# Operand slots at multiples of 128 bytes, the mixing ahead of the second value projection, and varied stationary offsets in four gate pairs

## The chip, the cores and the metric

The kernel runs on one core of a Trainium2 chip, in one launch. The metric is the device time of the launch in microseconds (us), the median of several executions. One further execution was recorded by the hardware profiler, and every row below is from it. TensorE is called PE, VectorE DVE, ScalarE ACT, GpSimd POOL, and SyncE SP; SP issues the DMAs.

## The reference

One layer of a hybrid model on T = 1024 tokens of width 1024, all in float32. `x @ w_in` gives the inputs of three branches: attention over compressed, selected and windowed keys (A), spatial gating (B), and a chunked mLSTM with four heads (C). What is around the change:

```python
def _spatial_gating(u, v, ln_g, ln_b, w_s, b_s):        # branch B
    u = jax.nn.gelu(u)
    v = _layernorm(jax.nn.gelu(v), ln_g, ln_b)
    v = v.reshape(bsz, t_len // CHUNK_B, CHUNK_B, G_B, CH_B)
    w = w_s * jnp.tril(jnp.ones((CHUNK_B, CHUNK_B), w_s.dtype))
    mixed = jnp.einsum('gts,bcsge->bctge', w, v) + b_s.T[:, :, None]
    return u * mixed.reshape(bsz, t_len, D_B)
...
# branch C: q, k through a causal convolution over 4 tokens, gates i and f per token,
# per head 8 chunks of 128 tokens, each with a carried state
...
g = jax.nn.sigmoid(m_g).reshape(bsz, t_len, N_BRANCH, D_MODEL)
merged = g[:, :, 0] * (y_a @ w_br_a[i]) + g[:, :, 1] * (y_b @ w_br_b[i]) + g[:, :, 2] * (y_c @ w_br_c[i])
r = ALPHA * x + merged @ w_out[i]
r = r + jax.nn.sigmoid(r @ ple_gate[i]) * (p[i] @ ple_w[i])
x = _layernorm(r, ln_g[i], ln_b[i])
```

## The kernel before

**Products.** Each float32 operand is split into a high part in a rounded matmul format (fp32r) and the remainder as a low part in the same format. A product of two operands is three matmuls: high by high, low by high, high by low. Each matmul has its own weight load, which runs beside the matmul ahead of it. The kernel has 7135 matmuls, most of them with a moving operand of 512 columns; the program names them by the line that issues them: L130 (projections, the products of the branches, and the output product), L139 (values and gates of the attention, 288 columns), L151 (projections in token order, 256 columns), L786 (Strassen products), L1050 and L1090 (last gate).

**Stages in order of time.** The attention with the projections woven into it takes the time to about 491 us. From there the values of branch B and branch C are projected by `proj_tok256` (L151): the first value projection (weights `wtm[0]`, `wtm[1]`, 384 matmuls) goes through a gelu into `vb`, the second (`wtm[2]`, `wtm[3]`, 384 matmuls) is copied to `vs` and stored to the DRAM scratch `v1scr` (L714, L716). In the same stretch the sums of x that Strassen's method needs (`xraw`, L652 to L658, with their split `split_op`, L643) and the gate recurrences of branch C are computed: `gi`, `gf`, `bc` (L670 to L677), a round trip through DRAM to lay out each chunk's last values (`lastv` to `lscr` to `lrow`, then the scan `mrow`, L689), another for `mp`, and three transposes of them on PE (L706). Then comes the mixing of branch B: L722 is a matmul for its bias, and eight chunks follow, each one with four matmuls (L741, two passes each in the records), four scaled additions on DVE from PSUM (L744) and four products with the gate in `yb` (L747). `yb` is stored to `ysc[1]`. Then 20 Strassen products follow from about 601 to 1040 us. Each is 7 products of 12 matmuls at L786, 84 in all, 1680 for the 20. The stationary operand of each is one slot of `sh` (high, L772, ACT) and `sl` (low, L773, DVE), the moving operand is a part of `xhs`/`xls` or of a sum. Of the 20, 12 are gate pairs (`mg_pair`), the last four of which (q = 8 to 11) come after the heads. The chunk recurrences of each head (L920 to L970) are woven into the others. The branch products, the output product, and the last gate end the kernel.

**Order.** The framework's scheduler takes instructions in the order in which the program was written as their priority, and each engine then runs its own list strictly in order, with semaphores between engines.

**Slots.** On-chip buffers are laid out one after another in the order in which pools are opened, each at a multiple of 32 bytes. `ident` takes 512 bytes of a partition, and `vec`, 53 columns of 4 bytes, takes 224 in its slot; so all later slots start 96 bytes past a multiple of 128. The `y` slots hold 1032 columns (`YW`, for the four columns of padding of the convolution), 4128 bytes, so each starts 32 bytes further in its line of 128 than the one ahead of it. Worked out from these sizes, the start within 128 bytes of the operands (moving, stationary) is:

| line | matmuls | moving | stationary |
|---|---|---|---|
| L130 | 1824 | 96 | 96 |
| L139 | 192 | 0 | 96 |
| L151 | 768 | 96 | 96 |
| L514, L515 (scores of the attention) | | 0 | 0 |
| L786 | 1680 | 96 | 0 |
| L1050 | 432 | 96 | 96 (342), 0 (72), 64 (18) |
| L1090 | | 32 or 64 or 96 | 96 or 32 |

Of the kernel before, what the change touches and what calls it, by code (L numbers as in the profile page):

```python
# [46 lines left out]
def hybrid_kernel(ctx, tc, xm, pT, wfm, wvg, wtm, cmpw1, cmpw2, cpos, vecs, sgwT, sgb,  # L47
# [579 lines left out]
    nc.gpsimd.affine_select(out=wT, in_=wT, pattern=[[0, 4], [1, P]], compare_op=OP.is_ge,
                            fill=0.0, base=0, channel_multiplier=-1)
    ones = pq.tile([P, P], F32, name="ones")
    vv.memset(ones, 1.0)  # L630
    bsb = pq.tile([P, 512], F32, tag="mt", bufs=1, name="bsb")
    nc.sync.dma_start(bsb, sgb.to_broadcast([P, 512]))
# [29 lines left out]


# [46 lines left out]
    v1scr = dr.tile([NH_C, P, NT, P], F32, name="v1scr")  # L710
    for wi in range(2):
        for i, po in enumerate(proj_tok256(wtm[2 + wi], xh, xl)):
            vs = pq.tile([P, 2, 2, P], F32, tag="vs", bufs=2, name="vs")
            nc.any.tensor_copy(out=vs.rearrange("p j a d -> p (j a d)"), in_=po)  # L714
            for a in range(2):
                nc.sync.dma_start(v1scr[2 * wi + a, :, 2 * i:2 * i + 2, :], vs[:, :, a, :])  # L716
    for m in range(2):
        right["T4"][m] = split_op(t4[m], xp, "x", 16)


# [514 lines left out]
```

## Time and profile before

| | |
|---|---|
| median of 3 executions | 1395.22 us (1393.98 to 1396.69) |
| profiled execution | 1394.37 us, its span 1392.6 us |
| PE busy | 1355.7 us, 97% of the span |
| DVE, ACT, POOL busy | 61%, 37%, 11% |
| chain that ended last | PE 85%, DVE 6%, DMA 3%, ACT 3%, issue 2% |

The span is that of the program in the trace; some 1.8 us of the execution's time lie around it. A busy PE counts a matmul from its start to its modelled end, and matmuls overlap, so the pace is read from one start to the next. The chain is followed back from the last instruction, from each to what released it; its shares say which engine the end waited for.

### The profile page before, as it was taken

The numbers are of one execution on the slowest core, as the hardware profiler recorded it, in microseconds if no ns is written. First come the engines' busy times: TensorE is split into PE (matmuls) and PEld (weight loads), VectorE is DVE, ScalarE is ACT, GpSimd is POOL, SyncE is SP. The second block draws the span as 40 slices with busy tenths as digits, with TensorE's granted clock in tenths as the row PEclk, the third lists the DMA queues.
The fourth block names the chain that finished last, engine by engine and source line by source line (L and its number), as shares of the span: only waits on it lengthen the run. The fifth ranks groups of instructions, "written<-read, shape, count | busy, mean of one in ns | idle before, by whom it ended". The sixth has DMA issues, their size and how long they took to land.

```text
span 1392.6 us, 18947 instructions
## 1 busy us (share of the span) xinstructions
PE 1355.7 (97%) x7135; PEld 1134.0 (81%) x7135; DVE 849.4 (61%) x1974; ACT 521.9 (37%) x1040; POOL 158.0 (11%) x181
## 2 busy tenths in 40 slices
PE   9999999999999998889999999999999999999997
PEld 7977888887888998868788787887878887888786
DVE  6236686436777557377776677766454546334755
ACT  6353434243342343135445355454452212223211
POOL 0011211101211100001001000010000344000312
PEclk9999999999999999999999999999999999999999
DMA  8131101111110042333222332235346543113211
GB/s 311 31 84 32 31 24 42 39 46 54 43 64 5 16 153 77 92 106 122 91 61 95 117 108 75 76 121 197 121 141 217 181 157 121 46 61 126 94 38 46
DMA packets 47931, 127.46 MB, mean 92 GB/s; under 512 B 5080, under 2 KB 16216, under 8 KB 47840
## 3 DMA queue, kind: packets, MB, share of 16 engines
q1 hardware_dynamic: 46880, 123.11, 26.8%
q0 software_dynamic: 960, 3.15, 1.0%
q8 instruction: 56, 0.92, 0.3%
q14 instruction: 35, 0.29, 0.1%
HBM read 101.00 MB, written 25.23 MB: 91 GB/s over the span
## 4 chain that ended last, share of the span: by engine, by line
PE 85%; DVE 6%; DMA 3%; ACT 3%; issue 2%; POOL 0%; SPq 0%; DVEq 0%; ACTq 0%; POOLq 0%
PE ps_pj L130 18%; PE ps_a L786 15%; PE ps_b L130 9%; PE ps_b L786 8%; PE ps_o L537 7%; PE ps_g L1050 5%; PE ps_c L786 4%; PE ps_st L514 2%; PE ps_pj L151 2%; PE ps_v L139 2%; PE ps_st L515 2%; PE ps_e L1090 2%; PE ps_st L151 1%; PE ps_s L493 1%; DMA xraw<-in_xm_dram 1%
## 5 line engine op out<-in xcount | busy, mean ns | idle before, releaser
L537 PEld LDWEIGHTS ps_o<-V,pt 128*128 128x128 f32 x912 | 117.6, 191 | 12.1 <-ACT pt L517 3.3
L130 PE MATMUL ps_pj<-xh,whi 128*128 128x512 f32 x288 | 115.5, 401 | 2.3 <-DVE QA L403 2.3
L537 PE MATMUL ps_o<-V,pt 128*128 128x65 f32 x912 | 116.6, 269 | 0.5 <-POOL pt L519 0.3
L130 PE MATMUL ps_pj<-xh,wlo 128*128 128x512 f32 x288 | 114.8, 398 | 0.0
L130 PE MATMUL ps_pj<-xl,whi 128*128 128x512 f32 x288 | 114.5, 398 | 0.0
L517 ACT ACTIVATE pt<-ps_st 128x512 f32<-128x512 f32 x114 | 65.4, 594 | 103.9 <-PE ps_st L515 96.7
L786 PE MATMUL ps_a<-op_hi,sl 128*128 128x512 f32 x240 | 95.2, 397 | 0.0
L786 PE MATMUL ps_a<-op_lo,sh 128*128 128x512 f32 x240 | 95.2, 396 | 0.0
L786 PE MATMUL ps_a<-op_hi,sh 128*128 128x512 f32 x240 | 94.7, 395 | 0.0
L773 DVE TENSOR_TENSOR sl<-ss,sh 128x512 fp32r<-128x512 f32 x80 | 54.8, 689 | 61.8 <-ACT sh L772 58.6
L93 ACT CAST whi<-wraw 128x1024 fp32r<-128x1024 f32 x46 | 48.2, 1048 | 82.7 <-PE ps_b L130 46.9
L130 PE MATMUL ps_b<-sp_hi,wlo 128*128 128x512 f32 x192 | 74.8, 390 | 1.3 <-DVE wlo L94 1.3
L94 DVE TENSOR_TENSOR wlo<-wraw,whi 128x1024 fp32r<-128x1024 f32 x46 | 61.7, 1342 | 22.6 <-ACT whi L93 18.4
L130 PE MATMUL ps_b<-sp_lo,whi 128*128 128x512 f32 x192 | 74.7, 389 | 0.0
L130 PE MATMUL ps_b<-sp_hi,whi 128*128 128x512 f32 x192 | 74.0, 390 | 0.0
L772 ACT CAST sh<-mraw 128x512 fp32r<-128x512 f32 x60 | 37.3, 622 | 82.6 <-PE ps_c L786 33.6
L1005 POOL TENSOR_TENSOR M<-M,gt 128x512 f32<-128x512 f32 x32 | 42.9, 1349 | 203.8 <-issue 174.3
L130 PEld LDWEIGHTS ps_pj<-xh,whi 128*128 128x128 f32 x288 | 54.2, 188 | 13.6 <-PE ps_pj L130 3.9
L130 PEld LDWEIGHTS ps_pj<-xl,whi 128*128 128x128 f32 x288 | 54.2, 188 | 9.8
L130 PEld LDWEIGHTS ps_pj<-xh,wlo 128*128 128x128 f32 x288 | 54.3, 189 | 9.0
L772 ACT CAST sh<-ss 128x512 fp32r<-128x512 f32 x80 | 49.6, 620 | 26.0 <-PE ps_b L786 25.3
L786 PEld LDWEIGHTS ps_a<-op_hi,sl 128*128 128x128 f32 x240 | 45.2, 188 | 11.0
(370 smaller groups left out, 3549.6 us busy)
## 6 DMA issues: line engine op xcount, KB each, us to landing
mraw<-in_wfm_dram SPq DMA_DIRECT2D x40, 512.0 KB, 3.6
gsc<-gt SPq DMA_DIRECT2D x24, 512.0 KB, 2.6
gt<-gsc SPq DMA_DIRECT2D x24, 512.0 KB, 4.1
wraw<-in_wfm_dram SPq DMA_DIRECT2D x18, 512.0 KB, 3.6
xraw<-in_xm_dram SPq DMA_DIRECT2D x14, 512.0 KB, 6.0
yraw<-ysc SPq DMA_DIRECT2D x12, 512.0 KB, 4.4
wraw<-in_wbr_dram SPq DMA_DIRECT2D x12, 512.0 KB, 4.4
wraw<-in_wtm_dram SPq DMA_DIRECT2D x8, 512.0 KB, 3.8
```

The source lines that it names most:

```text
L93: nc.scalar.copy(hi[:, c], raw[:, c])
L94: vv.tensor_sub(lo[:, c], raw[:, c], hi[:, c])
L130: mm(po[:M, :], lhsT=a[:, k, :], rhs=b(k, half), start=(i == 0), stop=(i == n - 1))
L139: mm(po[:, :n], lhsT=tok(a, k, tt), rhs=b[:, k % 4, :], start=(i == 0), stop=(i == tot - 1))
L151: mm(po, lhsT=tok(a, 4 * i + k, tt), rhs=b[:, k, :], start=(i == 0 and tt % 2 == 0 and k == 0 and j == 0), stop=(i == 1 and k == 3 and j = ...
L517: act(pt.rearrange("p h q -> p (h q)"), sp, AF.Exp)
L537: mm(po[:, h * 65:h * 65 + 65], lhsT=pt[:, h, :], rhs=V[:, j, vi, :], start=(first and h == 0), stop=last, skip_group_check=True)
L772: nc.scalar.copy(hi, src)
L773: vv.tensor_sub(lo, src, hi)
L786: mm(bank, lhsT=l[a][:, k, :], rhs=r[b], start=first and k == 0 and i == 0, stop=k == K - 1 and i == 2, skip_group_check=True)
L1005: nc.gpsimd.tensor_add(M[n][:, s], M[n][:, s], t[:, s])
L1050: mm(po[:, 0:n], lhsT=a[k][:, ts_], rhs=b[k][:, s], start=(k == 0 and i == 0), stop=(k == KT - 1 and i == 2))
```

## The change

The change has four parts. First, slots: `vec` is 64 columns wide, the convolution's buffers and `nb` fill whole slots of 4096 bytes, `sh` and `sl` have 544 columns and `ng4` 32. Worked out as above, every moving operand of L130, L151, L786 (L787 after it), L1050 and L1090 and every stationary one starts at 0 within 128 bytes, but for the part that follows; the scores of the attention start at 32 and 32, and L139 at 32 and 0. Second, offsets: in the four last gate pairs the stationary operand starts at 4, 8, 16, 32, 48, 64 or 96 bytes, by the product (`STARTS`, in elements of 4 bytes). Third, the convolution adds shifted slices (1021 to 1023 columns) in place of a padded buffer, and the denominators of the chunks go into a small buffer `dn` by a copy of one column on DVE, 32 of them in all. Fourth, the order of the text: the sums of x (`split_op` and what follows it) stand ahead of the first value projection, and the mixing stands ahead of the second.

```diff
-YW = 1032
+STARTS = dict(B11=4, T1=2, T2=8, B21=16, T3=24, B22=1, T4=12)
...
-    vec = cst.tile([P, 53], F32, name="vec")
+    vec = cst.tile([P, 64], F32, name="vec")
...
-    wT = pq.tile([P, 4, P], F32, name="wT")
-    nc.sync.dma_start(wT, sgwT)
...
-    vb = [pq.tile([P, 2, 512], F32, tag="yc", bufs=4, name="vb") for _ in range(4)]
-    for wi in range(2):
-        for i, po in enumerate(proj_tok256(wtm[wi], xh, xl)):
-            gelu2(vb[i][:, :, wi * 256:wi * 256 + 256], po.rearrange("p (t n) -> p t n", t=2), 512)
...
         right[n] = [(xhs[m + r][j], xls[m + r][j]) for r in range(2)]
 
+    wT = pq.tile([P, 4, P], F32, name="wT")
+    nc.sync.dma_start(wT, sgwT)
...
+    vb = [pq.tile([P, 2, 512], F32, tag="yc", bufs=4, name="vb") for _ in range(4)]
+    for wi in range(2):
+        for i, po in enumerate(proj_tok256(wtm[wi], xh, xl)):
+            gelu2(vb[i][:, :, wi * 256:wi * 256 + 256], po.rearrange("p (t n) -> p t n", t=2), 512)
...
-    v1scr = dr.tile([NH_C, P, NT, P], F32, name="v1scr")
-    for wi in range(2):
-        for i, po in enumerate(proj_tok256(wtm[2 + wi], xh, xl)):
...
     prs = pst("m", 2)
     mm(prs, lhsT=ones, rhs=wT.rearrange("p g t -> p (g t)"), start=True, stop=True)
...
     for i in range(4):
         nc.sync.dma_start(ysc[1][i], yb[i])
 
+
+    v1scr = dr.tile([NH_C, P, NT, P], F32, name="v1scr")
+    for wi in range(2):
+        for i, po in enumerate(proj_tok256(wtm[2 + wi], xh, xl)):
+            vs = pq.tile([P, 2, 2, P], F32, tag="vs", bufs=2, name="vs")
+            nc.any.tensor_copy(out=vs.rearrange("p j a d -> p (j a d)"), in_=po)
+            for a in range(2):
+                nc.sync.dma_start(v1scr[2 * wi + a, :, 2 * i:2 * i + 2, :], vs[:, :, a, :])
+    for m in range(2):
+        right["T4"][m] = split_op(t4[m], xp, "x", 16)
...
-        def left(src):
-            hi = pg_.tile([P, 512], F32R, tag="sh", bufs=3, name="sh")[:, 0:w]
-            lo = pg_.tile([P, 512], F32R, tag="sl", bufs=3, name="sl")[:, 0:w]
+        def left(src, at):
+            hi = pg_.tile([P, 544], F32R, tag="sh", bufs=3, name="sh")[:, at:at + w]
+            lo = pg_.tile([P, 544], F32R, tag="sl", bufs=3, name="sl")[:, at:at + w]
...
-            l = left(src)
+            l = left(src, starts.get(name, 0))
...
-        xq = [yp.tile([P, YW], F32, tag="y", bufs=YB, name="xpad") for _ in range(2)]
-        for t in xq:
-            nc.gpsimd.memset(t[:, 0:4], 0.0)
+        xq = [yp.tile([P, T], F32, tag="y", bufs=YB, name="xq") for _ in range(2)]
...
-        nb = yp.tile([P, NT, 129], F32, tag="y", bufs=YB, name="nb")
+        nb = yp.tile([P, NT, P], F32, tag="y", bufs=YB, name="nb")
+        dn = pq.tile([P, NT], F32, tag="dn", bufs=1, name="dn")
...
-            nc.scalar.copy(nb[:, c, :], pn[:, 0:129])
+            nc.scalar.copy(nb[:, c, :], pn[:, 0:P])
+            vv.tensor_copy(dn[:, c:c + 1], pn[:, P:P + 1])
...
     for q in range(8, 12):
-        mg_pair(q)
+        mg_pair(q, STARTS)
```

What it moves on the engines is seen at three places. The first is PE's list from the transposes of the recurrences to the first Strassen product; before, the second projection runs up to L722 and all of the mixing follows it:

```order
L706 MATMUL ps_m<-ident,gi 128x32
L151 MATMUL ps_pj<-whi,xh 128x256
...
L706 MATMUL ps_m<-ident,bc 128x32
L151 MATMUL ps_pj<-wlo,xh 128x256
L151 MATMUL ps_pj<-whi,xl 128x256
L706 MATMUL ps_m<-ident,gf 128x32
...
L151 MATMUL ps_st<-whi,xl 128x256
L722 MATMUL ps_m<-wT,ones 128x512
L741 MATMUL ps_m<-wT,vb 128x128 x32
L786 MATMUL ps_a<-xh,sh 128x512
```

In the same stretch of the list after the change, L711, L730 and L787 are what L722, L741 and L786 were:

```order
L706 MATMUL ps_m<-ident,gi 128x32
L711 MATMUL ps_m<-wT,ones 128x512
L151 MATMUL ps_pj<-whi,xh 128x256
...
L730 MATMUL ps_m<-wT,vb 128x128 x4
L151 MATMUL ps_st<-wlo,xh 128x256
...
L706 MATMUL ps_m<-ident,bc 128x32
...
L730 MATMUL ps_m<-wT,vb 128x128 x8
L151 MATMUL ps_pj<-wlo,xh 128x256
...
L151 MATMUL ps_st<-whi,xl 128x256
L787 MATMUL ps_a<-xh,sh 128x512
```

The eight chunks of the mixing now stand inside the second projection: 94 matmuls of L151 after L711 comes the first chunk, between chunks stand 6 to 18 more (two chunks stand together), and after the eighth come 210, the last 192 of which are the projection's second half of weights.

The second place is DVE's list ahead of `gi`, which the first transpose on PE reads. Before:

```order
L652 TENSOR_TENSOR xraw<-xraw 128x1024
L673 SCALAR_TENSOR_TENSOR gf<-gf,rt 32x128
L675 MEMSET rt 32x128
L654 TENSOR_TENSOR xraw<-xraw 128x1024
L643 TENSOR_TENSOR op_lo<-xraw,op_hi 128x1024
L655 TENSOR_TENSOR xraw<-xraw 128x1024
L676 SCALAR_TENSOR_TENSOR bc<-gf,rt 32x128
L174 SCALAR_TENSOR_TENSOR ge_a<-ge_a,ps_pj 128x512
L677 TENSOR_TENSOR gi<-gi,bc 32x128
```

After (L640 and L642 are what L652 and L654 were, L631 is L643; the two of x's sums ahead of these rows are left out):

```order
L631 TENSOR_TENSOR op_lo<-xraw,op_hi 128x1024
L643 TENSOR_TENSOR xraw<-xraw 128x1024
...
L94 TENSOR_TENSOR wlo<-wraw,whi 128x1024
L631 TENSOR_TENSOR op_lo<-xraw,op_hi 128x1024
...
L646 TENSOR_TENSOR xraw<-xraw 128x1024
L176 SCALAR_TENSOR_TENSOR vb<-ge_a,ps_pj 128x2x256
L174 SCALAR_TENSOR_TENSOR ge_a<-ge_a,ps_pj 128x512
L676 SCALAR_TENSOR_TENSOR bc<-gf,rt 32x128
L719 BN_STATS s_5335<-vb 128x6
...
L677 TENSOR_TENSOR gi<-gi,bc 32x128
```

From the first of x's sums (L652, L640) to `gi`, before has four passes over 1024 columns, one of 512 and three small ones; after has eight over 1024 (L640, L642, L643, L646, L94 and three of L631), five over 512 (L174, L176), one L719 and three small ones.

The third place is SP's list of DMAs at the end of the second projection. Before:

```order
L822 DMA mraw<-in_wfm_dram 128x1024
L716 DMA v1scr<-vs 128x2x128 x2
L756 DMA ysc_81<-yb 128x1024
```

After:

```order
L745 DMA ysc_84<-yb 128x1024
L823 DMA mraw<-in_wfm_dram 128x1024 x2
L754 DMA v1scr<-vs 128x2x128 x6
L823 DMA mraw<-in_wfm_dram 128x1024
L754 DMA v1scr<-vs 128x2x128 x2
L899 DMA V_6417<-v1scr 128x8x128
```

The last stores of `v1scr` now stand behind those of `yb`. The pool with `wT`, `vb` and `vs` (`pq`) closes behind them, and `sh`, `sl`, `ng4` and `V1` lie in the space that it frees; so the first `sh` waits for the last store out of `vs`, where it waited for the last use of the mixing's buffers.

## Rows read from the trace of the kernel before

**Rows 1.** The page, busy time, share of the span and instructions of each engine.
```profile
PE 1355.7 (97%) x7135; PEld 1134.0 (81%) x7135; DVE 849.4 (61%) x1974; ACT 521.9 (37%) x1040; POOL 158.0 (11%) x181
```

**Rows 2.** Timeline of PE, L130: start, duration (us), line, operation, tiles, shape.
```profile
1099.67 0.39 PE L130 MATMUL ps_b<-sp_lo,whi 128*128 128x512 f32 x1
...
1102.84 0.39 PE L130 MATMUL ps_b<-sp_hi,wlo 128*128 128x512 f32 x1
```

**Rows 3.** Timeline of PE, L786.
```profile
706.42 0.40 PE L786 MATMUL ps_b<-xh,sh 128*128 128x512 f32 x1
...
708.99 0.40 PE L786 MATMUL ps_b<-xl,sh 128*128 128x512 f32 x1
```

**Rows 4.** Timeline of PE, L1050.
```profile
1285.73 0.39 PE L1050 MATMUL ps_g<-gh,sp_hi 128*128 128x512 f32 x1
...
1290.82 0.40 PE L1050 MATMUL ps_g<-gl,sp_hi 128*128 128x512 f32 x1
```

**Rows 5.** Timeline of PE, L151 (256 columns).
```profile
500.08 0.28 PE L151 MATMUL ps_st<-whi,xl 128*128 128x256 f32 x1
...
503.20 0.28 PE L151 MATMUL ps_st<-wlo,xh 128*128 128x256 f32 x1
```

**Rows 6.** Timeline of PE, L139 (288 columns).
```profile
39.71 0.30 PE L139 MATMUL ps_v<-wh,xh 128*128 128x288 f32 x1
...
41.98 0.29 PE L139 MATMUL ps_v<-wh,xl 128*128 128x288 f32 x1
```

**Rows 7.** Timeline of PE, the attention's L514 and L515.
```profile
480.69 0.39 PE L515 MATMUL ps_st<-QB,KBs 128*128 128x512 f32 x1
...
481.15 0.40 PE L515 MATMUL ps_st<-QB,KBs 128*128 128x512 f32 x1
```

**Rows 8.** Timeline of DVE, 517 to 545 us; in brackets the idle time and releaser.
```profile
517.33 1.22 DVE L652 TENSOR_TENSOR xraw<-xraw 128x1024 f32<-128x1024 f32 x1 [3.10 <-DMA xraw<-in_xm_dram]
...
520.00 1.20 DVE L643 TENSOR_TENSOR op_lo<-xraw,op_hi 128x1024 fp32r<-128x1024 f32 x1
...
521.13 1.21 DVE L655 TENSOR_TENSOR xraw<-xraw 128x1024 f32<-128x1024 f32 x1
...
522.60 0.65 DVE L174 SCALAR_TENSOR_TENSOR ge_a<-ge_a,ps_pj 128x512 f32<-128x512 f32 x1
...
523.18 0.27 DVE L677 TENSOR_TENSOR gi<-gi,bc 32x128 f32<-32x128 f32 x1
...
533.61 0.13 DVE L681 COPY lastv<-cm 32x1 f32<-32x1 f32 x1
...
541.19 0.17 DVE L689 TENSOR_TENSOR_SCAN mrow<-lrow 4x8 f32<-4x8 f32 x1 [1.82 <-DMA lrow<-lscr]
...
544.31 1.00 DVE L737 TENSOR_SCALAR vb<-vb,mv,rs_y 128x512 f32<-128x512 f32 x2
```

**Rows 9.** Window: us, PE busy (x), granted clock, DMA share, GB/s.
```profile
546.50:553.30 6.80, 5.05 (x22) 0.50 0.41 121
```

**Rows 10.** Timeline of PE, 527 to 601 us.
```profile
527.65 0.24 PE L706 MATMUL ps_m<-ident,gi 32*128 32x32 f32 x1
...
548.25 0.31 PE L706 MATMUL ps_m<-ident,bc 32*128 32x32 f32 x1 [4.58 <-ACT bc L701]
...
585.34 1.16 PE L741 MATMUL ps_m<-wT,vb 128*128 128x128 f32 x8 [0.41 <-DVE mt L744]
...
593.53 1.16 PE L741 MATMUL ps_m<-wT,vb 128*128 128x128 f32 x8 [0.89 <-DVE mt L744]
...
600.92 0.80 PE L786 MATMUL ps_a<-xh,sh 128*128 128x512 f32 x1 [4.18 <-ACT sh L772]
```

**Rows 11.** Timeline of ACT at 581 and 600 us.
```profile
581.71 0.58 ACT L714 COPY vs<-ps_st 128x512 f32<-128x512 f32 x1 [2.29 <-PE ps_st L151]
...
600.25 0.62 ACT L772 CAST sh<-mraw 128x512 fp32r<-128x512 f32 x1 [17.95 <-DVE yb L747]
```

**Rows 12.** DMA issues, 582.3 to 583.3 us: count, KB each, us to landing.
```profile
v1scr<-vs SPq DMA_DIRECT2D x2, 128.0 KB, 3.8
```

More of the change, by code (lines that the diff above doesn't have):

```diff
@@ L233, in hybrid_kernel @@
     nc.sync.dma_start(ident, identc)
-    nc.sync.dma_start(vec, vecs)
+    nc.sync.dma_start(vec[:, 0:53], vecs)
     pa_ctx = ExitStack()
@@ L624, in hybrid_kernel @@
     pq = pq_ctx.enter_context(tc.tile_pool(name="pq", bufs=1))
-    wT = pq.tile([P, 4, P], F32, name="wT")
-    nc.sync.dma_start(wT, sgwT)
[L627 to L632, printed above, removed]
-    vb = [pq.tile([P, 2, 512], F32, tag="yc", bufs=4, name="vb") for _ in range(4)]
-    for wi in range(2):
-        for i, po in enumerate(proj_tok256(wtm[wi], xh, xl)):
-            gelu2(vb[i][:, :, wi * 256:wi * 256 + 256], po.rearrange("p (t n) -> p t n", t=2), 512)
     def split_op(src, pl_, tg, bf):
@@ L661, in hybrid_kernel @@
         right[n] = [(xhs[m + r][j], xls[m + r][j]) for r in range(2)]
+    wT = pq.tile([P, 4, P], F32, name="wT")
+    nc.sync.dma_start(wT, sgwT)
+    nc.gpsimd.affine_select(out=wT, in_=wT, pattern=[[0, 4], [1, P]], compare_op=OP.is_ge,
+                            fill=0.0, base=0, channel_multiplier=-1)
+    ones = pq.tile([P, P], F32, name="ones")
+    vv.memset(ones, 1.0)
+    bsb = pq.tile([P, 512], F32, tag="mt", bufs=1, name="bsb")
+    nc.sync.dma_start(bsb, sgb.to_broadcast([P, 512]))
+    vb = [pq.tile([P, 2, 512], F32, tag="yc", bufs=4, name="vb") for _ in range(4)]
+    for wi in range(2):
+        for i, po in enumerate(proj_tok256(wtm[wi], xh, xl)):
+            gelu2(vb[i][:, :, wi * 256:wi * 256 + 256], po.rearrange("p (t n) -> p t n", t=2), 512)
     gi = pq.tile([32, P], F32, name="gi")
@@ L708, in hybrid_kernel @@
     vv.tensor_scalar_mul(cols[:, 2, :], pc_[:, 64:96], CS)
-    v1scr = dr.tile([NH_C, P, NT, P], F32, name="v1scr")
-    for wi in range(2):
-        for i, po in enumerate(proj_tok256(wtm[2 + wi], xh, xl)):
[L713 to L718, printed above, removed]
     prs = pst("m", 2)
@@ L761, in hybrid_kernel, with strassen @@
     pq = pg_
-    ng4 = pg_.tile([P, 4], F32, name="ng4")
-    vv.tensor_scalar_mul(ng4, vec[:, C_NG:C_NG + 4], 0.25)
-    def strassen(raw0, raw1, K, right, done):
+    ng4 = pg_.tile([P, 32], F32, name="ng4")
+    vv.tensor_scalar_mul(ng4[:, 0:4], vec[:, C_NG:C_NG + 4], 0.25)
+    def strassen(raw0, raw1, K, right, done, starts={}):
         w = K * P
         a11, a12, a21, a22 = raw0[:, 0:w], raw0[:, w:2 * w], raw1[:, 0:w], raw1[:, w:2 * w]
-        def left(src):
-            hi = pg_.tile([P, 512], F32R, tag="sh", bufs=3, name="sh")[:, 0:w]
-            lo = pg_.tile([P, 512], F32R, tag="sl", bufs=3, name="sl")[:, 0:w]
+        def left(src, at):
+            hi = pg_.tile([P, 544], F32R, tag="sh", bufs=3, name="sh")[:, at:at + w]
+            lo = pg_.tile([P, 544], F32R, tag="sl", bufs=3, name="sl")[:, at:at + w]
             nc.scalar.copy(hi, src)
@@ L814, in hybrid_kernel, with strassen_fm @@
     rawn = [0]
-    def strassen_fm(f0, f1, done):
+    def strassen_fm(f0, f1, done, starts={}):
         tg = ("wraw", "whi")[rawn[0] % 2]
@@ L822, in strassen_fm, with mg_pair @@
             nc.sync.dma_start(t, wfm[f])
-        strassen(raw[0], raw[1], 4, right, done)
-    def mg_pair(q):
+        strassen(raw[0], raw[1], 4, right, done, starts)
+    def mg_pair(q, starts={}):
         gt = [wp.tile([P, T], F32, tag="wlo", bufs=WB, name="gt") for _ in range(2)]
@@ L832, in done @@
             act(gt[i][:, j * 512:j * 512 + 512], bank, AF.Tanh, scale=0.5)
-        strassen_fm(FM["mg"] + 2 * q, FM["mg"] + 2 * q + 1, done)
+        strassen_fm(FM["mg"] + 2 * q, FM["mg"] + 2 * q + 1, done, starts)
         for i in range(2):
@@ L857, in tap @@
                 return vec[:, C_CW + 4 * i + j:C_CW + 4 * i + j + 1]
-            act(r, x[:, 4:4 + T], AF.Identity, scale=tap(3), bias=vec[:, C_CB + i:C_CB + i + 1])
-            for j in range(3):
-                stt(out=r, in0=x[:, 1 + j:1 + j + T], scalar=tap(j), in1=r, op0=OP.mult, op1=OP.add)
+            act(r, x, AF.Identity, scale=tap(3), bias=vec[:, C_CB + i:C_CB + i + 1])
+            for d in (3, 2, 1):
+                stt(out=r[:, d:T], in0=x[:, 0:T - d], scalar=tap(3 - d), in1=r[:, d:T], op0=OP.mult, op1=OP.add)
             for half in range(2):
@@ L953, in hybrid_kernel @@
                 C1 = Cn
-        dn = pq.tile([P, NT], F32, tag="dn", bufs=1, name="dn")
-        stt(out=dn.unsqueeze(2), in0=nb[:, :, P:P + 1], scalar=-1.0, in1=nb[:, :, P:P + 1], op0=OP.mult, op1=OP.max)
+        stt(out=dn, in0=dn, scalar=-1.0, in1=dn, op0=OP.mult, op1=OP.max)
         vv.tensor_max(dn, dn, cols[:, 1, 8 * h:8 * h + 8])
```

2 lines of the change are left out of this document (1 added, 1 removed).

## The prediction

> **What bounds the kernel now.** The page comes first: PE is busy for 97% of the span [rows 1], and the chain that ended last is mostly PE. So two things count: the pace of a matmul behind the one ahead of it, and the few places where PE waits. The pace is read from the timelines, as starts of matmuls far from any interruption, because durations overlap. At L130, with both operands 96 bytes past a multiple of 128, 14 steps take 3.17 us, 226.4 ns each [rows 2]. At L786, same shape, moving operand at 96 and stationary at 0, 11 steps take 2.57 us, 233.6 ns [rows 3]. L1050 in its part with unequal starts takes 5.09 us for 22, 231.4 ns [rows 4]. L151, 256 columns and both at 96, takes 3.12 us for 26, 120.0 ns [rows 5]. From L130 and L151 one column costs (226.4 - 120.0) / 256 = 0.416 ns, and some 13 ns are fixed; the fixed part at L786 is 20. The reader is to see that the two commonest kinds of matmul differ by 7 ns with nothing but their addresses (and the program around them) apart.
>
> The waits come next, in the timeline from 527 to 601 us. PE stands for 4.58 us before a transpose of `bc` [rows 10], and behind it a window of 6.8 us has a granted clock of 0.50 with 5.05 us of PE work in it [rows 9], so the low clock costs 5.05 / 2 = 2.5 us. The mixing goes from chunk to chunk in steps of (593.53 - 585.34) / 4 = 2.05 us, each begun by a wait for DVE's additions, and the first Strassen matmul waits 4.18 us for its `sh`, to start at 600.92 [rows 10].
>
> **Slots.** 1680 matmuls at L786 now read both operands from 0. Of these, 336 are in the four varied pairs. Of the other 1344, about 1150 stand in long runs; there I take the full step from L786 to L130, 233.6 - 226.4 = 7.2, taken as 6.8 because the last digit of the rows (10 ns over 11 and 14 steps) leaves it open by about 1: 7.8 us. The some 196 in between the chunk recurrences are interrupted every few matmuls; for them I take a third, 2.5 ns each, 0.5 us. L1050 and L1090 have about 170 with unequal starts, at 231.4 - 226.4 = 5.0 ns (5.5 with the slower ones at L1090): 0.9 us. L130 and L151 were equal and stay equal: nothing, which holds if equality and not the value 96 is what counts. The attention's operands go from 0 and 0 to 32 and 32, equal as before: nothing. L139 has its operands 96 apart before, in the other direction, and its 17 steps take 2.27 us [rows 6], 133.5 ns; less 288 columns at 0.416 this is 13.7 fixed. So a moving operand at 0 with a stationary one at 96 costs what equal starts cost: the slow case is a moving operand at 96 with a stationary one at 0, or it needs more columns. In either reading 0 with 0 should be fast, but no long run here shows it: the attention's three at 0 and 0 are 0.46 us apart over two steps [rows 7], 230 ns, behind other shapes and not settled. This is the step with the least support. Its bounds are 0 (the pace is the same) and the same 7.2 ns on all 1680, 12.1 us.
>
> **Varied offsets.** 336 matmuls with stationary starts from 4 to 96 bytes, moving at 0. Bounds per matmul: 6.8 ns saved (as L130), or 3.5 lost (half the step again, on top of L786's own); so 2.3 saved to 1.2 lost. By L139's row the 96 should be fast; I take 0.9 saved.
>
> **The Trainium skill's rule here.** Rows 2 and 3 show 226.4 and 233.6 ns for one shape. The Trainium skill says in "TensorE: Matmul & The Clock Gate", section "Step-by-step: what each phase is for", that PE has two independent read ports, one for the moving operand and one for weight loads, so that loading the next weights doesn't take bandwidth from the running matmul; and "SBUF — State Buffer", section "Specifications (TRN2)", gives cachelines of 16 bytes, for which 0, 32 and 96 are alike. By both the starts shouldn't matter, and the time would be 1392.8. The trace disagrees as far as the two rows go, but it can't say that the addresses are the reason.
>
> **The order.** I follow it engine by engine.
> - *gi.* Before, from the landing of the last `xraw` at 517.33 to `gi` at 523.18, DVE does four passes over 1024 columns, 1.13 us from start to start (520.00 to 521.13), a half pass of 0.58 (522.60 to 523.18), and small ones [rows 8]. After, the order has eight full passes, five half ones, one L719 (priced as a half) and the small ones (5.85 - 4 x 1.13 - 0.58 = 0.75): 9.0 + 3.5 + 0.75 = 13.3 us, so `gi` begins at about 530.6 and ends at 530.9. PE comes to its transpose at 527.65 [rows 10] and waits about 3.2 us. Queued behind it are L711 and the second projection.
> - *First chunk.* From there L711 (0.9) and 94 of L151 at 0.12 bring PE to the first L730 at about 543.2. Its `vb` needs the statistics of all chunks and the square root. On DVE these stand partly behind `mrow`, which waits for a round trip through DRAM: `lastv` 533.61, `mrow` 541.19 [rows 8], 7.6 us. With `lastv` at about 533.3 `mrow` comes at 540.8; the statistics left over (2.3, four half passes), the root (3.1, from 541.19 to 544.31) and one normalization (0.5) give 546.8. PE waits 3.6 us. Since this wait ends at 546.8 whatever the one for `gi` does, the first is absorbed in it.
> - *To the end of the projection.* From the first L730 PE has eight chunks of 1.16 [rows 10] and a change of form each (1.2), 290 matmuls at 0.12, and two transposes: about 44.8 us, so it ends at 591.6. DVE needs 2.05 a chunk and 0.54 for the next normalization, 2.6 in all, beside 2.6 to 2.9 on PE, so it hides, just; if it didn't, each chunk would cost PE some tenths, up to 2 us. The 4.58 us wait for `bc` and the mixing's waits for DVE are what goes.
> - *First Strassen product.* What is late next is the last `vs`. Its copy takes 0.58 [rows 11], its store lands 3.8 us after issue [rows 12] (SP's load of `mraw` ahead of it is issued by then), and `sh` takes 0.62 [rows 11]; with the steps between, 5.6 us. L787 begins at about 597.3 instead of 600.92: 3.6 us gained. `ng4` and `V1` wait for the same store, but nothing on PE asks for them for many us.
>
> Bounds: without the wait at the first chunk 3.6 more, 7.2 gained; with the clock falling behind both waits as it did before, twice 2.5, 1.4 lost. The waits are shorter than the 4.58 us that went ahead of the low clock. I take half of one fall, 1.2: **2.4 us gained**.
>
> **Small edits.** The 32 copies of one column on DVE (0.13 us by the `lastv` row [rows 8], 4 us in all) lie beside the Strassen matmuls; DVE is 61% busy. If that cover were gone, the chunk's wait would grow by 0.13, 4 us in all; I take 0.1 lost. The convolution without padding saves two POOL fills per head that PE doesn't wait for: nothing.
>
> **Sum.** 7.8 + 0.5 + 0.9 + 0.9 + 2.4 - 0.1 = 12.4 us. Against the profiled execution (1394.37, span 1392.6 and 1.8 around it) this is 1382.0; the median of three is 0.85 above the profiled one, and against it I say **1382.5**, its own range 1376 to 1388.
>
> **Rivals.** About 0.2%, 2.8 us, is what a measurement of this kernel can tell from no change; so faster is below 1392.4 and slower above 1398.0.
> - *The starts don't matter* (0.13). L786 differs from L130 by its surroundings (ACT writing `sh` and DVE `sl` beside it, other banks), and only the order's 2.4 and the odd 0.1 remain: 1395.2 - 2.4 = 1392.8. For it: L139, unequal and not slow. Against it: L1050, far from the Strassen products, is slow too where its starts are unequal. The two rules of the Trainium skill would make this one.
> - *0 with 0 is a slow pair* (0.11). The attention's 230 ns would be its pace, or up to 231. Then L130 loses 1824 x 4.6 = 8.4 us, L151 768 x 4.6 = 3.5, L1050 and L1090 360 x 4.6 = 1.7; L786 gains 1680 x 2.6 = 4.4, the order 2.4: 6.8 us lost, about **1402**. It decides where the pace p of 0 with 0 passes 229.6 ns: 2952 (p - 226.4) = 1680 (233.6 - p) + 2400. For it: those are the only rows with 0 and 0. Against it: three matmuls behind another shape are no settled run.
> - *Aligned starts take away part of the fixed 13 ns as well* (0.07). If 5 of it went on all 3600 and more in long runs, 18 us more, some 1364. For it: nothing but that the fixed part has to come from somewhere; L139 with its moving operand at 0 has it in full, which is against it.
> - *A new wait eats the gain* (0.07): the mixing's DVE work turns into PE's pace, or the clock falls more often in the woven stretch: 1388 to 1398.
>
> **How the numbers follow.** The forecast has 0.62. The range leaves out the pair of far cases, 0.18: from 1374 (the forecast with all bounds good: 3.6 for the missing wait, 1.4 for the offsets, 1.2 for the clock, 2 for 7.2 ns everywhere) to 1396. Faster: 0.62, half of the first rival, 0.07, and part of the last: 0.77. Slower: the second rival and little else, 0.11. Same: 0.12.
>
> **What would show it.** Right: steps of 227 ns at L787 in the 16 plain products, against 231 to 237 in the four varied pairs, by product; L1050 at 227 throughout; L130 still 226 to 227. PE waiting about 3 us at `gi` and 3 to 4 at the first L730 (at 547), none at `bc`, no DVE waits in the mixing above some tenths, L787 first at 597. Wrong: L787 still at 233, which is the first rival; L130 at 230, the second; L151 below 115, the third; a clock of 0.50 in more than one window between 530 and 600, or chunks over 3.5 us apart, the last.

## The result, and the profile after

The changed kernel takes 1380.99 us (median of 4, 1379.31 to 1382.15), the kernel before 1394.99 on the same chip: a ratio of 0.9897 [0.988, 0.9915], 14.0 us faster. The prediction was 1382.5. The time came out, but not from where the prediction had it.

The page after (span; PE busy; chain by engine), beside [rows 1]:

```profile
span 1379.7 us, 18957 instructions
...
PE 1348.5 (98%) x7135; PEld 1133.2 (82%) x7135; DVE 848.6 (62%) x2006; ACT 521.9 (38%) x1040; POOL 157.9 (11%) x173
...
PE 86%; DVE 6%; DMA 3%; ACT 2%; issue 1%; POOL 0%; SPq 0%; DVEq 0%; ACTq 0%; POOLq 0%
```

The span is 12.9 us shorter with the same instructions on PE. Where they went is read from three starts: the first Strassen product, its end, and the end of the last gate. Before, the first product starts at 600.92 [rows 10] and the branch products behind the last one at 1039.79; after, at 593.30 and 1026.09. So 7.6 us are won ahead of the Strassen products, 438.9 - 432.8 = 6.1 in them; behind them 0.9 are lost.

**Ahead of them.** The timeline of PE after, with the idle time and its releaser in brackets, answers [rows 10]:

```profile
530.07 0.24 PE L706 MATMUL ps_m<-ident,gi 32*128 32x32 f32 x1 [1.82 <-DVE lastv L682]
...
544.75 0.46 PE L730 MATMUL ps_m<-wT,vb 128*128 128x128 f32 x2 [0.61 <-DVE vb L726]
...
587.33 0.28 PE L151 MATMUL ps_st<-whi,xl 128*128 128x256 f32 x1
...
593.30 0.80 PE L787 MATMUL ps_a<-xh,sh 128*128 128x512 f32 x1 [5.69 <-ACT sh L773]
```

The transpose of `gi` waits 1.8 us, the first chunk of the mixing (L730) 0.6, and nothing waits at `bc`. The projection's last matmul starts at 587.33, and the first Strassen matmul stands 5.69 us for its `sh`. The chain behind this on DVE, answering [rows 8]:

```profile
529.74 0.27 DVE L677 TENSOR_TENSOR gi<-gi,bc 32x128 f32<-32x128 f32 x1
...
532.17 0.13 DVE L681 COPY lastv<-cm 32x1 f32<-32x1 f32 x1
...
538.60 0.16 DVE L689 TENSOR_TENSOR_SCAN mrow<-lrow 4x8 f32<-4x8 f32 x1 [1.54 <-DMA lrow<-lscr]
...
544.06 1.00 DVE L726 TENSOR_SCALAR vb<-vb,mv,rs_y 128x512 f32<-128x512 f32 x2
```

`gi` starts at 529.74 where 530.6 was predicted, `mrow` at 538.60 (540.8), the first `vb` at 544.06. The windows (us, PE busy, granted clock, DMA share, GB/s) show what followed each of three waits:

```profile
530.80:533.90 3.10, 3.10 (x15) 0.57 0.01 0
593.30:599.20 5.90, 5.62 (x12) 0.50 0.30 89
1281.00:1286.00 5.00, 5.00 (x15) 0.66 0.30 120
```

The low clock behind `gi`'s wait made PE late, and this lateness took the place of the wait for `vb`, which is why that is only 0.6 us. Behind the 5.69 us wait nothing covers the low clock: it costs 5.62 / 2 = 2.8 us. That isn't all new. The kernel before has a low clock there too, besides the one of [rows 9]:

```profile
597.70:604.50 6.80, 3.58 (x8) 0.50 0.72 277
```

There it costs 3.58 / 2 = 1.8 us. So the first Strassen product takes 22.73 us after and 21.50 before, and 19.44 where the clock doesn't fall (e11, below). The third fall, behind a wait of 2.1 us in the last gate, wasn't there before.

**In them.** The long runs of L787, answering [rows 3], first and last of 12:

```profile
641.10 0.40 PE L787 MATMUL ps_a<-op_hi,sh 128*128 128x512 f32 x1
...
643.67 0.39 PE L787 MATMUL ps_a<-op_lo,sh 128*128 128x512 f32 x1
```

11 steps in 2.57 us: 233.6 ns, as before. Over the 11 steps inside a product the undisturbed ones without varied offsets have 230.6 to 234.5, where before they had 232.5 to 234.3. The step to 226.4 ns on which most of the predicted gain rested is not there, although every operand now starts at a multiple of 128. L1050, in the part of [rows 4], did go to 226 to 227 (2.26 us for 10 steps):

```profile
1275.08 0.39 PE L1050 MATMUL ps_g<-gl,sp_hi 128*128 128x512 f32 x1
...
1277.34 0.39 PE L1050 MATMUL ps_g<-gh,sp_lo 128*128 128x512 f32 x1
```

The gain inside the Strassen products is mostly elsewhere: in the four of them that share PE with a head's chunk recurrences. Before, the first of these takes from 661.88 to 692.42 (below), 30.54 us; after 655.31 to 684.57, 29.26. All four: 122.2 before, 116.8 after. The other 15 gain 1.9 us together, and the first one loses 1.2.

### The profile page after: what moved, and what is told of

Read it like the earlier page. It is cut to its first block, busy times and chain, and to the rows that moved or that the text cites. A ratio compares the mean times of both kernels' runs of the same rounds, so it can differ in the third digit from the quotient of the medians.

```text
span 1379.7 us, 18957 instructions
## 1 busy us (share of the span) xinstructions
PE 1348.5 (98%) x7135; PEld 1133.2 (82%) x7135; DVE 848.6 (62%) x2006; ACT 521.9 (38%) x1040; POOL 157.9 (11%) x173
## 4 chain that ended last, share of the span: by engine, by line
PE 86%; DVE 6%; DMA 3%; ACT 2%; issue 1%; POOL 0%; SPq 0%; DVEq 0%; ACTq 0%; POOLq 0%
PE ps_pj L130 18%; PE ps_a L787 15%; PE ps_b L130 9%; PE ps_b L787 8%; PE ps_o L537 7%; PE ps_g L1050 5%; PE ps_c L787 3%; PE ps_st L514 2%; PE ps_pj L151 2%; PE ps_v L139 2%; PE ps_st L515 2%; PE ps_e L1090 2%; PE ps_st L151 1%; PE ps_s L493 1%; DMA xraw<-in_xm_dram 1%
## 5 line engine op out<-in xcount | busy, mean ns | idle before, releaser
L130 PE MATMUL ps_pj<-xh,whi 128*128 128x512 f32 x288 | 115.6, 401 | 2.3 <-DVE QA L403 2.3
L537 PE MATMUL ps_o<-V,pt 128*128 128x65 f32 x912 | 116.6, 269 | 0.5 <-POOL pt L519 0.3
L130 PE MATMUL ps_pj<-xh,wlo 128*128 128x512 f32 x288 | 114.7, 398 | 0.0
L130 PE MATMUL ps_pj<-xl,whi 128*128 128x512 f32 x288 | 114.5, 398 | 0.0
L787 PE MATMUL ps_a<-op_hi,sl 128*128 128x512 f32 x240 | 95.2, 397 | 0.0
L787 PE MATMUL ps_a<-op_hi,sh 128*128 128x512 f32 x240 | 95.1, 396 | 0.0
L787 PE MATMUL ps_a<-op_lo,sh 128*128 128x512 f32 x240 | 95.1, 396 | 0.0
L130 PE MATMUL ps_b<-sp_hi,wlo 128*128 128x512 f32 x192 | 74.8, 390 | 1.3 <-DVE wlo L94 1.3
L130 PE MATMUL ps_b<-sp_lo,whi 128*128 128x512 f32 x192 | 74.7, 389 | 0.0
L130 PE MATMUL ps_b<-sp_hi,whi 128*128 128x512 f32 x192 | 74.0, 389 | 0.0
L94 DVE TENSOR_TENSOR wlo<-wraw,whi 128x1024 fp32r<-128x1024 f32 x46 | 61.5, 1337 | 13.5 <-ACT whi L93 9.3
L130 PEld LDWEIGHTS ps_pj<-xh,whi 128*128 128x128 f32 x288 | 54.2, 188 | 13.6 <-PE ps_pj L130 3.9
L130 PEld LDWEIGHTS ps_pj<-xl,whi 128*128 128x128 f32 x288 | 54.2, 188 | 10.0
L130 PEld LDWEIGHTS ps_pj<-xh,wlo 128*128 128x128 f32 x288 | 54.3, 188 | 9.1
L787 PEld LDWEIGHTS ps_a<-op_hi,sh 128*128 128x128 f32 x240 | 45.2, 188 | 10.8
```

What stands on the lines that cost most here:

```text
L94: vv.tensor_sub(lo[:, c], raw[:, c], hi[:, c])
L130: mm(po[:M, :], lhsT=a[:, k, :], rhs=b(k, half), start=(i == 0), stop=(i == n - 1))
L537: mm(po[:, h * 65:h * 65 + 65], lhsT=pt[:, h, :], rhs=V[:, j, vi, :], start=(first and h == 0), stop=last, skip_group_check=True)
```

## The experiments

Every kernel ran beside the kernel before on its chip; medians are given with that of before, and the ratio has its 95% interval.

**Order alone (e1)**: the change with the slots, offsets, convolution and `nb` of before. Two places of what differs from the change:

```diff
-STARTS = dict(B11=4, T1=2, T2=8, B21=16, T3=24, B22=1, T4=12)
+YW = 1032
...
-    vec = cst.tile([P, 64], F32, name="vec")
+    vec = cst.tile([P, 53], F32, name="vec")
```

> The slots, the offsets, the convolution and dn are those of before; only the text's new order stands. My theory of the trace after: the order brought the first Strassen product from 600.92 to 593.3 us, some 8 us with the 0.5 us by which that trace began later, and the pace at L786 comes from addresses. Then this runs at 1387 us (1386 to 1388) and L786 keeps 233.4 ns. Rival: the pace of the Strassen products has to do with what runs beside them, which the order changes too: then L786 falls to some 232 ns here and the time comes near 1381. As the prediction had it, the order was worth 2.4 us: 1392.6.

1390.19 against 1395.75, ratio 0.9958 [0.9946, 0.9971]: 5.6 us. The first Strassen product starts at 593.64, the long runs stay at 233 ns, and the heads' stretches at 122.8 us. The waits of PE from 500 to 610 us (total, times, longest):

```profile
PE ps_a L787 <- ACT sh L773: 5.5, 1, 5.5
PE ps_m L706 <- DVE lastv L682: 1.8, 1, 1.8
PE ps_m L730 <- DVE vb L726: 0.8, 1, 0.8
PE ps_a L787 <- DVE sl L774: 0.3, 1, 0.3
```

It is 3 us short of my theory's 1387: the first Strassen product comes 7.3 us sooner than before, but 1.5 are given back in the Strassen products, 0.9 of it in the first one, behind the 5.5 us wait. The rival falls: order doesn't change the pace.

**Slots alone (e2)**: the order of before with all the rest of the change. Two places of what differs from the kernel before:

```diff
-            nc.scalar.copy(nb[:, c, :], pn[:, 0:129])
+            nc.scalar.copy(nb[:, c, :], pn[:, 0:P])
+            vv.tensor_copy(dn[:, c:c + 1], pn[:, P:P + 1])
...
     for q in range(8, 12):
-        mg_pair(q)
+        mg_pair(q, STARTS)
```

> The order of before with the slots, the offsets and the small edits of the change. My theory: the Strassen products gain 6.1 us, as between the two traces, and nothing else does: 1389 us (1388 to 1390), the wait of 4.6 us for bc and the first Strassen product at 601 us are there as before. As the prediction had it: 10 us gained, 1385. Rival, order and slots only help together: 1395.

1386.63 against 1395.75, ratio 0.9933 [0.9921, 0.9946]: 9.1 us, more than I expected. The Strassen products take 431.2 us, 7.7 less, and 1.5 come from the last gate: 0.9 of it is a shorter wait (1.0 for 1.9), and the low clock that the gate has after the change isn't there. Of the 7.7, 5.5 are in the heads' stretches (116.7); "slots alone" holds the small edits too, and e9 tells them apart. With e1 it makes 14.7 us, the change 14.0: the parts add up.

**No varied offsets (e3)**

```diff
-        mg_pair(q, STARTS)
+        mg_pair(q)
```

> The change without the varied offsets: the four last gate pairs are as the other sixteen products. My theory, from the trace after: a Strassen product of the last four takes 19.4 to 19.5 us and one of the undisturbed others 19.45 to 19.57, so the offsets are worth nothing: 1381 us (1380.5 to 1381.5). The prediction's 0.9 us saved by them compares with slots at 226.7 ns, which they don't have. If the offsets cost what the prediction's lower bound said, 1.2 us, or helped by 2.3, this shows 1379.8 or 1383.3.

1381.73 against 1395.75, ratio 0.99 [0.9887, 0.9914]. The last four Strassen products take 77.92 us together, with the offsets 77.89. The offsets are worth nothing.

**Slots of 2048 bytes (e4)**: as e3, with

```diff
-            hi = pg_.tile([P, 544], F32R, tag="sh", bufs=3, name="sh")[:, at:at + w]
-            lo = pg_.tile([P, 544], F32R, tag="sl", bufs=3, name="sl")[:, at:at + w]
+            hi = pg_.tile([P, 512], F32R, tag="sh", bufs=3, name="sh")[:, at:at + w]
+            lo = pg_.tile([P, 512], F32R, tag="sl", bufs=3, name="sl")[:, at:at + w]
```

> As e3, with the slots of sh and sl 512 columns wide again, 2048 bytes, where 544 columns make 2176 bytes and move each slot by 128 within a line of 512. All operands still start at multiples of 128 bytes. Within 512 bytes the moving operand and the stationary one then agree in the products of B11, B21, B22 and T4 (960 matmuls) and are 128 apart in T1, T2 and T3 (720). Theory A, the starts must agree within more than 128 bytes: the 960 run at 226.7 ns, the 720 at 231 or more: some 5 us less than e3, 1376. Theory B, agreement within 128 bytes is all and what is left at L787 comes from the work beside it: no change from e3, 231.9 ns in all products, 1381.

1378.29, ratio 0.987 [0.9855, 0.9885]. The products B11 and T4 run at 226.7 ns, B21 and B22 at 228, T1, T2 and T3 at 233 to 234. So theory A, with 3.4 us of the 5 expected: the matmuls between the recurrences gain nothing (the heads' stretches take 116.7 us in e3 and 116.8 here), B21 and B22 take their first three steps at 231 to 233 ns, and T1, T2 and T3, where neither `sh` nor `sl` agrees now, are 0.4 to 1.4 ns slower. Theory B falls.

**All within 512 (e5)**: as e4, and

```diff
-    vec = cst.tile([P, 64], F32, name="vec")
+    vec = cst.tile([P, 128], F32, name="vec")
...
-    cols = pt_.tile([P, 3, 32], F32, name="cols")
+    cols = pt_.tile([P, 4, 32], F32, name="cols")
...
-    ng4 = pg_.tile([P, 32], F32, name="ng4")
+    ng4 = pg_.tile([P, 128], F32, name="ng4")
```

> As e4, with cols, vec and ng4 padded to 512 bytes, so that moving and stationary operand agree within 512 bytes in all of L130, L151, L787, L1050 and L1090. Theory A (agreement within 512, or a part of it over 128): every Strassen product at 226.7 ns in its long runs, T1, T2 and T3 too, which e4 has at 233: 720 x 6 ns = 4.3 us less than e4, 1374. Theory B (agreement within 128 is all): as e3, 1381. Rival: T1 to T3 are slow because ACT and DVE make their operands from sums just then: as e4, 1378.

1374.79 against 1394.33, ratio 0.986 [0.9847, 0.9874]. The timeline at the end of T1 and in T2, which e4 has at 233 ns:

```profile
640.33 0.39 PE L787 MATMUL ps_b<-op_lo,sh 128*128 128x512 f32 x1
...
642.82 0.39 PE L787 MATMUL ps_a<-op_hi,sl 128*128 128x512 f32 x1
```

11 steps in 2.49 us, 226.4 ns. The 14 long Strassen products without recurrences take 267.7 us together, 271.1 in e4, 273.8 after the change and 275.6 before. So the rival falls: ACT and DVE make the operands beside T1 to T3 here as well, and the pace is 226.4 ns all the same.

**Offsets, far and near (e6, e7)**: as e5 with slots of 640 columns, a fixed step for each product in all 20, and one buffer less for `ss` and `cp`. The fence has e6; in e7 `STARTS` stays as in the change.

```diff
-STARTS = dict(B11=4, T1=2, T2=8, B21=16, T3=24, B22=1, T4=12)
+STARTS = dict(B11=0, T1=8, T2=16, B21=32, T3=64, B22=96, T4=48)
...
-            hi = pg_.tile([P, 512], F32R, tag="sh", bufs=3, name="sh")[:, at:at + w]
+            hi = pg_.tile([P, 640], F32R, tag="sh", bufs=3, name="sh")[:, at:at + w]
...
-            l = left(src, starts.get(name, 0))
+            l = left(src, STARTS[name])
```

> As e5, but the stationary operand of each product lies a fixed step behind the moving one within 512 bytes: B11 0, T1 32, T2 64, B21 128, T3 256, B22 384, T4 192 bytes, in all 20 Strassen products (slots of 640 columns, one buffer less for the sums and the kept banks). It is a table of pace against offset, not a time. Theory A with 512: 226.7 ns at 0 alone, 231 to 234 at the others. With 256: 226.7 at 0 and 256, as 324 matmuls of L1050 before have it (256 apart, 226.9). Theory B: 226.7 at 0, 128, 256 and 384, slow at 32, 64 and 192.

> As e6 with small steps: B11 16, T1 8, T2 32, B21 64, T3 96, B22 4, T4 48 bytes. Theory A: no step is at 226.7; the pace is between 229 and 236 by the step. If the lines of 16 bytes that the Trainium skill gives in SBUF - State Buffer, section Specifications (TRN2), were what counts, 16, 32, 48, 64 and 96 would be at 226.7 and 4 and 8 slower.

The times of single runs are 1381.76 and 1383.03. The timeline of e6 has B21 (128 bytes apart) and behind it T3 (256 apart), first and last of 8 each:

```profile
625.33 0.39 PE L787 MATMUL ps_c<-xh,sl 128*128 128x512 f32 x1
...
626.96 0.40 PE L787 MATMUL ps_c<-xl,sh 128*128 128x512 f32 x1
...
627.88 0.39 PE L787 MATMUL ps_a<-op_hi,sh 128*128 128x512 f32 x1
...
629.47 0.39 PE L787 MATMUL ps_a<-op_hi,sl 128*128 128x512 f32 x1
```

7 steps at B21 take 1.63 us, 232.9 ns; at T3 1.59, 227.1. Mean ns from start to start over the 11 steps inside a product, with the settling at its begin; each figure is the median of the undisturbed Strassen products:

```
bytes apart   0      4      8      16              32     48     64     96     128    192    256    384
ns            228.7  232.1  231.0  226.7 or 233.5  232.9  233.5  233.5  233.5  232.9  233.4  227.7  232.9
```

So the period is 256 bytes: 0 and 256 are fast, 128 and 384 slow, and no product is slow by itself, since in e5 all seven are fast at 0. At 16 bytes 12 of the 15 undisturbed products settle at 226.7 and three at 233.5; each of the three is the first behind a head's stretch, and why they differ isn't shown. The lines of 16 bytes in SBUF that the Trainium skill gives (SBUF — State Buffer, section Specifications (TRN2)) don't order this: 32 and 96 are slow. Of the other rule that the prediction named, in TensorE: Matmul & The Clock Gate, section Step-by-step: what each phase is for, that loading the next weights takes no bandwidth from a running matmul: where the starts agree nothing here speaks against it. Where they don't, a step is up to 7 ns longer by nothing but the two starts; whether the weight load is what lengthens it no run shows.

**Stores apart, on e5 (e8)**

```diff
-            vs = pq.tile([P, 2, 2, P], F32, tag="vs", bufs=2, name="vs")
+            vs = tp.tile([P, 512], F32, tag="ge_a", bufs=2, name="vs").rearrange("p (j a d) -> p j a d", j=2, a=2)
```

> As e5, and vs, from which the second value projection is stored, lies in the ge_a slots instead of the pool that closes; so sh no longer waits for the last store. My theory: in the trace after, PE stands 5.7 us before the first Strassen product for that store and then runs 5.9 us at the low clock; without the wait the product starts within 0.5 us of the projection's end: 5.2 to 5.7 us less than e5, and up to 2.5 more if the low clock goes too: 1367 (1365 to 1369). Rival: another use of the pool (wT, vb, mt) or the load of mraw ends as late, and nothing changes: 1374.

1363.93 against 1394.33, ratio 0.978 [0.9767, 0.9794]: 10.9 us less than e5, more than I expected, and the best version, 30 us below before. Between the two profiled executions it is 7.8 us. The first Strassen product starts 7.1 us sooner: 5.7 are the wait, and the rest goes with the clock, which doesn't fall behind the first chunk's wait in this execution. The product itself takes 19.07 us for 21.80, since the low clock behind the wait is gone too. The last gate gives back 2.5, with a longer wait (2.4 us for 1.2) and a low clock behind it.

**The copy of the denominators alone (e9)**: the kernel before with the lines below; `nb` loses its last column, and what read it reads `dn`.

```diff
-            nc.scalar.copy(nb[:, c, :], pn[:, 0:129])
+            nc.scalar.copy(nb[:, c, :], pn[:, 0:P])
+            vv.tensor_copy(dn[:, c:c + 1], pn[:, P:P + 1])
```

> The kernel before with one edit: the 32 copies of the denominators on DVE with the narrower copy on ACT; slots, starts and the text's order are those of before. In the traces each stretch with a head's chunk recurrences takes 30.5 us before and in e1, 29.1 in e2 and in the trace after, and the list of PE has more Strassen matmuls between the small ones there. My theory: the copy changes the scheduler's order, and that is the gain: four stretches with 1.4 us less, 1389.5 us (1388.5 to 1390.5). Rival: the small matmuls gain from their weights starting at multiples of 128 bytes; then nothing changes here, 1395. As the prediction had it, the copies cost 0.1 to 4 us: 1395 to 1399.

1389.9 against 1396.5, ratio 0.995 [0.9935, 0.9966]: 6.6 us by one edit that the prediction priced at a loss of 0.1. The heads' stretches take 116.6 us. PE's order in one of them, one letter for each matmul of the recurrences (S L920, t L926, W L938, C L940, u L947) and a dot for each of L786; first before and e1, then e9, e2 and after:

```
St...S...tWuS.tW.SCutSWt...CuSWtCuSWtCuSW.Cu..WCu.W...C
St...S...tWuS.t.WSCutS..Wt.CuS..WCutS.WCt.u.WSCu...WCu...WC
```

The timeline of before, with both ends of the stretch and one pair of the recurrences in it:

```profile
661.88 0.48 PE L786 MATMUL ps_a<-xh,sh 128*128 128x512 f32 x1
...
668.90 0.49 PE L938 MATMUL ps_n<-V,Wt 128*128 128x129 f32 x2
...
669.29 0.33 PE L926 MATMUL ps_k<-ident,k 128*128 128x128 f32 x1
...
692.42 0.40 PE L786 MATMUL ps_a<-xh,sh 128*128 128x512 f32 x1
```

And of e9:

```profile
664.18 0.48 PE L786 MATMUL ps_a<-xh,sh 128*128 128x512 f32 x1
...
671.52 0.41 PE L939 MATMUL ps_n<-V,Wt 128*128 128x129 f32 x2
...
671.76 0.39 PE L941 MATMUL ps_n<-C,qe 128*128 128x129 f32 x2
...
693.38 0.39 PE L786 MATMUL ps_a<-xh,sh 128*128 128x512 f32 x1
```

661.88 to 692.42 is 30.54 us, 664.18 to 693.38 is 29.20. One L938 (two records; L939 in e9) takes 0.39 us to the next start where small matmuls stand behind one another, and 0.24 where Strassen matmuls stand ahead of it. The views name no wait there, but the weight loads (PEld) of before show short ones:

```profile
668.50 0.30 PEld L920 LDWEIGHTS ps_cs<-q,k 128*128 128x128 f32 x2
...
668.59 0.27 ACT L941 COPY nb<-ps_n 128x129 f32<-128x129 f32 x1 [1.35 <-PE ps_n L940]
...
668.90 0.30 PEld L938 LDWEIGHTS ps_n<-V,Wt 128*128 128x128 f32 x2
...
669.29 0.14 PEld L926 LDWEIGHTS ps_k<-ident,k 128*128 128x128 f32 x1
```

The loads of L920 end at 668.80 and that of L938 starts at 668.90, just behind ACT's copy out of `ps_n`, which ends at 668.86; L926 comes 0.09 us late in the same way. A small matmul that waits for nothing takes 0.11 us to the next start in both kernels. Over the four stretches the steps between small matmuls are 6.7 us longer than that before, 3.1 in e9: 3.5 of the 5.6 us that the stretches gain. In e9 a Strassen matmul runs in many of these places, so that PE has work while ACT or DVE finish. Another 1.3 are won at the transposes of `nb` at the stretch's end (L970). Starts play no part in it: the unhindered step is the same, and the kernels with other slots (e2, after, e10) have e9's order and its time.

**Agreement at 96 (e10)**: as e5 with

```diff
-    vec = cst.tile([P, 128], F32, name="vec")
+    vec = cst.tile([P, 120], F32, name="vec")
```

> As e5, with vec 120 columns wide, so that all slots start 96 bytes past a multiple of 512; moving and stationary operands still agree. Theory A, only the agreement counts: 226.7 ns at L787, each head's stretch 29.1 us, the time of e5, 1375. Rival, the multiple of 128 itself counts: L787 at 231 to 234 and 1383; or the small matmuls alone lose by it, 1.4 us in each head's stretch: 1380.

1374.16 against 1396.5, ratio 0.984 [0.9825, 0.9855], and the heads' stretches at 116.6 us. The timeline in a long run, 11 steps in 2.50 us:

```profile
640.33 0.39 PE L787 MATMUL ps_a<-xh,sl 128*128 128x512 f32 x1
...
642.83 0.39 PE L787 MATMUL ps_b<-op_hi,sh 128*128 128x512 f32 x1
```

227 ns at operands that all start at 96 within 128 bytes. (Worked out from the sizes, `ident` and 480 bytes of `vec`, that is 480 past a multiple of 512, not 96 as the expectation says; they agree all the same.) The multiple of 128 in the change's name plays no part; the agreement does.

**Stores apart, on the change (e11)**: the edit of e8 on the changed kernel.

> The change as it is, with vs in the ge_a slots only: what the wait before the first Strassen product costs in the change. In the trace after it is 5.7 us, and the 5.9 us that follow at the low clock cost half of that, 2.9. My theory: both go, 8.3 us less than the change: 1372.7 (1371.5 to 1374). If the low clock comes from something else than the wait, 5.4 less: 1375.6. If the wait only changes its name (the load of mraw), 1381.

1371.55 against 1396.5, ratio 0.9823 [0.981, 0.9836]: 9 to 10 us less than the change, by the medians on two chips or by the two ratios. The first Strassen matmul follows the projection's last at its pace, and a window behind it is at the full clock:

```profile
589.46 0.28 PE L151 MATMUL ps_st<-whi,xl 128*128 128x256 f32 x1
...
589.58 0.39 PE L787 MATMUL ps_a<-xh,sh 128*128 128x512 f32 x1
```

```profile
590.00:595.00 5.00, 5.00 (x23) 1.00 0.63 157
```

Not all of it is the stores. Between the two profiled executions (9.3 us) the first Strassen product starts 3.7 us sooner, because here the clock falls for 6.8 us behind the first chunk's wait, where in the change's execution it fell for 3.4 us behind `gi` and a later wait hid that; the first product takes 19.44 us for 22.73; and the last gate is 2.1 us shorter, with a shorter wait (1.4 us) and without the low clock that the change's execution has there, which no part of the edit touches.

## Why the prediction came out, point by point

| term | predicted, us gained | measured |
|---|---|---|
| long runs at L787, 7.8, and between recurrences, 0.5 | 8.3 | 1.9 |
| L1050 and L1090 | 0.9 | 0.6 (e2, less the shorter wait); lost to a low clock after |
| varied offsets | 0.9 | 0.1 (e3) |
| order | 2.4 | 5.6 (e1) |
| small edits | -0.1 | 5.6 in the heads' stretches (e9), 6.6 by its medians |
| sum | 12.4 | 14.0, that of the medians; the rows are of different executions |

- **Slots**: the step that failed. "0 with 0 should be fast" took equality within 128 bytes from [rows 2] and [rows 3]. The operands of L130 were equal within 512 as well, and the rows couldn't tell the two. A slot of 544 columns has 2176 bytes, 8.5 times 256, and three of them lie between `sh` and `sl`: so, worked out from the sizes, the high and the low part of a product are always 128 apart within 256, and one of them disagrees with the moving operand. The prediction counted addresses only within 128. Its bound of 0 and the rival "the starts don't matter" were both nearer for this term, yet the mechanism, a pace set by the two starts, was right: with agreement within 256 every long run takes the step (e5). Between the recurrences it brings nothing: the heads' stretches take 117.1 us in e5. L1050 did, since its operands, by the sizes of their slots, agree there.
- **The second and third rival** are out: L130 keeps 227, 0 with 0 runs at 226.4 in e5 as 96 with 96 does in e10, and nothing goes below the 13 ns. Of the fourth there is one sign, the low clock in the last gate; the mixing's DVE work stays hidden.
- **Small edits**: failed. The prediction weighed the 32 copies as work on DVE (0.15 us each after) and found cover for them. What came with them was another list of the scheduler for PE, in which fewer small matmuls wait for ACT and DVE (e9). PE's order was read only around the projection, where the text had moved.
- **Order**: the mechanism was right, the size off. `gi` and the first `vb` came 1 and 2 us sooner than worked out (`lastv` at 532.17 and a shorter round trip to `mrow`, 6.4 us where 7.6 were taken), the two waits are 1.8 and 0.6 where 3.2 and 3.6 were said, and the projection ends 4 us sooner. "What is late next is the last `vs`" held to 0.3 us: 5.85 from the end of the projection to L787, 5.6 predicted. Half a fall of the clock was taken; in the profiled execution one behind `gi` was absorbed, one behind the 5.69 us wait cost 2.8, and one in the last gate was new. The sum had no term for the fall that the kernel before has at 597.7 us, 1.8 us in its first Strassen product. Which wait the clock falls behind differs between executions of one order: in e3 and e4 PE waits 2.6 and 2.1 us at the first chunk, the clock falls there for 6.8 us, and the first Strassen product starts at 597.6 and 596.3, where the prediction had 597.3 and the change's execution 593.3. So the 7.6 us won ahead of the Strassen products in that one are partly its luck; the medians of e1 have 5.6 for the order in all.
- **The time** came out by luck: the slots' error of 6 us one way met the small edits' 6 and the order's 3 the other way. Nor does the sum give the 1382.5 that was said: 12.4 from the median of 1395.22 is 1382.8.

## What to carry to other kernels

When two kinds of matmul of one shape have two paces, work out the starts of both operands for a larger period than the one in the change's name before a gain is put on them, and let one run tabulate pace against offset. After any edit that adds or takes an instruction, compare the order of every stretch that a scheduler fills, not only the one that was moved. A wait that PE has alone can cost more than its length, since the clock may fall behind it (2.8 us behind 5.69 after the change): ask which buffer's last reader it is, and put that buffer where nobody waits for it (e11: of its 9 to 10 us some 7 come ahead of and in the first Strassen product).

## What the runs showed of the hardware that was not expected

A matmul of 512 columns settles at 226.7 ns where the starts of moving and stationary operand agree within 256 bytes and at 231 to 234 where they don't (e5, e6, e10); 16 bytes apart it settles at either 226.7 or 233.5. What in the chip makes the period 256 was not tried. And waits of PE as short as 1.8 and 2.1 us were followed by a stretch at a granted clock below 1.00 in some executions and not in others: in e5 PE waited 2.4 us at the first chunk, up to 544.28, and the window behind it had a clock of 0.70; in e8 it waited 2.5 us, up to 544.46, and the same window had 1.00:

```profile
545.00:550.00 5.00, 5.00 (x29) 0.70 0.04 10
545.00:550.00 5.00, 5.00 (x42) 1.00 0.05 11
```
